# Branch projections of an encoder layer: sums on VectorE, branches joined by an accumulating transfer, weights' parts one product ahead, operands six ahead

## The chip, the cores and the metric

The kernel runs on one core of one Trainium2 chip. The metric is the device time of one execution in microseconds (us); for several executions the median stands. A core has five engines that run side by side, each strictly in its own order: TensorE (PE in the profile) multiplies matrices, VectorE (DVE) and ScalarE (ACT) work element by element, GpSimd (POOL) does so too but can't read the matrix results, and SyncE (SP) issues transfers. Transfers (DMA) can also be issued by ScalarE and GpSimd. Matrix results land in PSUM banks; everything else lies in SBUF tiles of 128 partitions.

## The reference

One encoder layer of width 1024 is applied to two groups (prompt and sample) of 512 tokens each, with the same weights, in float32. After a common input projection there are two branches: a bidirectional mLSTM whose gated output is projected by `w_mo`, and latent attention whose output is projected by `w_ao`. Both are merged by gates and projected once more:

```
y_m = (jax.nn.sigmoid(o) * hm.astype(x.dtype)) @ w_mo
...
y_a = mla_attention(q_nope, q_rope, k_nope, k_rope, va) @ w_ao
...
g_m, g_a = jnp.split(jax.nn.sigmoid(gm), 2, axis=-1)
x = x + (g_m * y_m + g_a * y_a) @ w_out
```

Then follow a normalisation, a SwiGLU feed-forward network (2816 wide) with residual, a gated embedding and a last normalisation.

## The kernel before

Activations lie transposed: one tile holds 128 channels of the 512 tokens of one group, so a group's activation of width 1024 is 8 tiles. Float32 products are made of three matmuls: every operand is split into a high part (a ScalarE cast to fp32r) and a low part (VectorE: the value less its high part, `lo_of`, line 152), and high x high, high x low and low x high are accumulated.

The branch projections, the feed-forward's gate and up projections and its down projection use a scheme of **seven products in place of eight** for a 2 x 2 block product. The four weight blocks are two halves of the contraction by two output tiles; the four operands are two halves of the contraction by the two groups: a and b are the lower half of group 0 and 1, c and d the upper half. The products are called P1, P2, P7, P6, P5, Q4 and P3. Some need sums of operands (`Ops.part`, lines 799 to 819: P7 = b - d, P6 = P7's less a, P5 = a - b, Q4 = P6's plus c, or c - a - d where P6's tile is gone) and sums of weight blocks (`Seven.weights`, lines 861 to 881: P7, P6 and P3, on GpSimd, partly in place). Each product is 12 pairs of weight load and matmul (lines 894 to 896; four tiles of contraction, three matmuls each). `Ops.need` splits the operands of one product; `wsplit` (lines 840 to 845) splits a weight part into one of five buffers, which go round. Results gather in three banks: b1 (P1, P6, P5, P3 one upon the other, copied out by ScalarE between, line 929), b0 (P2) and b2 (P7, Q4). `outputs` (line 923) forms the four result tiles of a quad after P2, P5, Q4 and P3 and hands each to `put`.

`chain` (line 899) writes down the order of products: quad i's P6, P5, Q4, P3 with quad i+1's P1, P2, P7 between them. At each place it asks for operands of this product and the `look` ones after it, makes the quads of this and the next product (which issues their weights' loads from ScalarE, line 855), and emits the product, which first makes its weights' parts. Two chains are run: one of eight quads for the branches (four of `mo` with operands `hops`, then four of `ao` with operands `oops`; line 1018, 862.7 to 1027.8 us of the profile), and one of the feed-forward (`head=True`, from 1154.5 us).

A planner sets each engine's order: it goes over the program with simulated times, and what is emitted earlier has the higher priority among the instructions that are ready. On the chip each engine then keeps that order, whatever the true times are. Where `pinned` is set the order of the text is kept.

For the branches: `put_z` (line 993) multiplies an mLSTM result by its gate and stores it to DRAM (`z1d`); `put_y` (line 1002) loads z back, loads the attention's gate into the tile y, makes y = (y + 1) * t (line 1007) and adds z (line 1008), both on VectorE. Then the sixteen y tiles are halved and split (lines 1026 and 1028), and the output projection (`out_proj`, `proj1`, lines 181 to 183) reads them tile 0 to 7 per group. The operands' sums of `hops` and `oops` run on GpSimd, but for P7's on VectorE. Those of `hops` for P1, P2, P7 and P6 are partly made during the last attention heads (`HOPS`, line 980).

Of the kernel before, what the change touches and what calls it, by code (L numbers as in the profile page):

```python
# [11 lines left out]
ALU = mybir.AluOpType  # L12
# [50 lines left out]
def encoder_kernel(ctx: ExitStack, tc: tile.TileContext, a):  # L63
# [21 lines left out]
    V, S, E, GP = (Engine(e) for e in (nc.vector, nc.scalar, nc.tensor, nc.gpsimd))  # L85
# [277 lines left out]
    for d in range(2):  # L363
        st = R("tr", "mst")
        nc.sync.dma_start(st[:, 0:P], a["mask"][d])
        m = MC.pool.tile([P, P], F32R, name=f"mask{d}")
# [9 lines left out]
    lf, u, z, q = dense("lf"), dense("u"), dense("z"), dense("q")  # L376
# [40 lines left out]
    for i in range(NB):  # L417
        c = slice(i * P, (i + 1) * P)
        V.tensor_tensor_scan(
            out=M[:, c], data0=A[0][:, c], data1=A[0][:, c], initial=mprev[:, i : i + 1], op0=ALU.max, op1=ALU.max  # L420
# [4 lines left out]
    for d in range(1, NB):  # L425
        GP.tensor_copy(out=A[d][:, (NB - d) * P : T], in_=A[0][:, (NB - d) * P : T])
        for j in range(NB - d):
            e = (j + d) * P - 1
            V.tensor_scalar(
                out=A[d][:, j * P : (j + 1) * P],  # L430
                in0=A[d - 1][:, j * P : (j + 1) * P],
# [341 lines left out]
    def load(src, sl=EV, tag="bk", n="ld"):  # L773
        t = sl(tag, n)
        nc.sync.dma_start(t, src)
        return t
# [70 lines left out]
    class Seven:  # L847


        def __init__(self, srcs, kh, ops, out):  # L850
            n = kh * P
            st = []
            for sl, src in zip((WP, WX) if wsn[0] % 4 < 2 else (WX, WP), srcs):
                t = sl("wst", "wst", F32, (P, 1024))
                S.dma_start(t[:, : 2 * n], src)
                st += [t[:, 0:n], t[:, n : 2 * n]]
            wsn[0] += 1
            self.st, self.n, self.kh, self.ops, self.out = st, n, kh, ops, out
            self.bk = {}

        def weights(self, name):
            n, (a11, a12, a21, a22) = self.n, self.st
# [17 lines left out]
                src = a12  # L880
            return wsplit(src)

        def product(self, name):
            whi, wlo = self.weights(name)
            b, first = {"P1": ("b1", 1), "P6": ("b1", 0), "P5": ("b1", 0), "P3": ("b1", 0), "P2": ("b0", 1),
                        "P7": ("b2", 1), "Q4": ("b2", 0)}[name]
            if first:
                self.bk[b] = bank(b)
            bk = self.bk[b]
            sk = dict(skip_group_check=True)  # L890
            for k in range(self.kh):
                c = slice(k * P, (k + 1) * P)
                hi, lo = self.ops.x[name][k]
                E.matmul(bk, whi[:, c], hi, start=bool(first) and k == 0, stop=False, **sk)  # L894
                E.matmul(bk, whi[:, c], lo, start=False, stop=False, **sk)  # L895
                E.matmul(bk, wlo[:, c], hi, start=False, stop=k == self.kh - 1, **sk)  # L896
            self.out(name, self.bk)

    def chain(quads, head=False, look=4):

        order = [(0, n) for n in ("P1", "P2", "P7")]
        if head:
            order = [(0, "P1"), (0, "P2"), (1, "P1"), (1, "P2"), (0, "P7"), (0, "P6"), (0, "P5"), (0, "Q4"), (1, "P7"), (0, "P3")]
        for i in range(1 if head else 0, len(quads)):
            for n in ("P6", "+P1", "P5", "+P2", "Q4", "+P7", "P3"):
                if n[0] != "+":
                    order.append((i, n))
                elif i + 1 < len(quads):
                    order.append((i + 1, n[1:]))
        made = {}  # L910

        def make(i):
            if i not in made:
                made[i] = quads[i][1]()

        for at, (q, n) in enumerate(order):
            for i, m in order[at : at + look + 1]:
                quads[i][0].need(m)
            for i, _ in order[at : at + 2]:
                make(i)  # L920
            made[q].product(n)

    def outputs(put):
# [23 lines left out]
    def load4(src):  # L947
        t = ev4("ld")
        nc.sync.dma_start(t, src)
        return t  # L950
# [6 lines left out]
        raws[0] += 1  # L957
        return load(hzd[g][k], *stage[raws[0] % 4])

    hops = Ops(hraw, None, lambda n: V if n == "P7" else GP)  # L960
    hops.tmp = lambda: None
    units = [(n, [k]) for k in range(4) for n in ("P1", "P2", "P7", "P6")]

# [29 lines left out]
    def put_z(c):  # L993
        def put(at, t):
            cc, g = c + 4 * at[0], at[1]
            m = load4(tmd[g][cc])
            V.scalar_tensor_tensor(out=m, in0=m, scalar=1.0, in1=t, op0=ALU.add, op1=ALU.mult)
            nc.sync.dma_start(z1d[g][cc], m)

        return put  # L1000

    def put_y(c):
        def put(at, t):
            cc, g = c + 4 * at[0], at[1]
            z = load4(z1d[g][cc])
            y = load(tad[g][cc], late["OP"] if c == 0 else X2, "sg" if c == 0 else "x")
            V.scalar_tensor_tensor(out=y, in0=y, scalar=1.0, in1=t, op0=ALU.add, op1=ALU.mult)
            V.tensor_tensor(out=y, in0=y, in1=z, op=ALU.add)
            yr[g][cc] = y

        return put

    oops = Ops(lambda g, k: load(ozd[g][k], X2, "x"), lambda: late["OP"]("ev", "t"), lambda n: V if n == "P7" else GP)

    def pair(kind, c, ops, put):
        return ops, lambda: Seven([a["w8"][W8[f"{kind}{i}"]] for i in (c, c + 4)], 4, ops, outputs(put))

    chain([pair("mo", c, hops, put_z(c)) for c in range(4)] + [pair("ao", c, oops, put_y(c)) for c in range(4)])


    y = [[None] * KD for _ in range(G)]
# [402 lines left out]
```

## Time and profile before

| | us |
|---|---|
| median of 3 runs | 1911.53 (1911.05 to 1914.97) |
| the profiled execution | 1912.25 |
| its span | 1910.5 |
| busy: TensorE / its weight loads | 1845.7 / 1534.8 |
| busy: VectorE, ScalarE, GpSimd | 1240.0, 878.6, 474.4 |

The span runs from the first to the last instruction of the profiled execution. In a row of the timeline stand start, length, engine, line, operation, tiles written and read (out<-in), count, and in brackets how long the engine was idle before and what ended it. In a row of the waits stand who waited for whom, the sum, the number of waits and the longest. In the table by stage, busy time and number of instructions stand for each engine, then the granted clock of TensorE, the share of the DMA engines and their rate. A group's row has its number of instructions, busy time, mean in ns, and the idle time before it by what ended it. Matmuls overlap, so their busy time says less than how far apart they start.

### The profile page before, as it was taken

How to read it: one execution, taken by the hardware profiler on the slowest of the kernel's cores; microseconds unless marked ns; L12 is line 12 of the kernel's file. 1: busy time of each engine (PE TensorE's matmuls, PEld its weight loads, DVE VectorE, ACT ScalarE, POOL GpSimd, SP SyncE). 2: the span in 40 equal slices, each digit the busy share in tenths (PEclk: the TensorE clock that was granted, in tenths of full speed). 3: DMA queues.
4: the chain of work that ended last, by engine and by line, in shares of the span. 5: the costliest groups of instructions: out<-in, count | busy, mean ns of one | idle time of the engine just before them, and what ended most of it. 6: DMA issues, size and time to landing. Idle time of an engine off the chain costs nothing.

```text
span 1910.5 us, 24510 instructions
## 1 busy us (share of the span) xinstructions
PE 1845.7 (97%) x8840; PEld 1534.8 (80%) x8840; DVE 1240.0 (65%) x2134; ACT 878.6 (46%) x1711; POOL 474.4 (25%) x353
## 2 busy tenths in 40 slices
PE   7999999999999999899999988999999999999997
PEld 6898998988888877678777876888888887878886
DVE  7656575836555567976897576444444558778757
ACT  5255555644445566784444345333333344434442
POOL 3000000100000001242540023666565654232100
PEclk9999999999999999999999998999999999999999
DMA  4111101112253123346555331233222336534232
GB/s 163 51 45 34 56 34 56 34 67 72 81 187 121 50 69 122 105 144 215 150 189 179 106 121 64 102 109 112 94 98 93 130 136 222 170 118 143 88 127 88
DMA packets 97881, 207.58 MB, mean 109 GB/s; under 512 B 10656, under 2 KB 21280, under 8 KB 97760
## 3 DMA queue, kind: packets, MB, share of 16 engines
q1 hardware_dynamic: 85664, 163.03, 25.5%
q10 hardware_dynamic: 12096, 43.00, 6.9%
q8 instruction: 69, 1.13, 0.2%
q14 instruction: 52, 0.43, 0.1%
HBM read 151.89 MB, written 54.10 MB: 108 GB/s over the span
## 4 chain that ended last, share of the span: by engine, by line
PE 83%; DVE 9%; issue 3%; ACT 2%; DMA 1%; POOL 1%; SPq 0%; ACTq 0%; DVEq 0%; POOLq 0%
PE b L894 12%; PE b L896 12%; PE b L895 12%; PE mm L181 8%; PE mm L183 8%; PE mm L182 8%; PE nm L580 3%; DVE xl L152 2%; PE mm L79 2%; PE mm L495 2%; PE mm L497 2%; PE mm L496 2%; DVE wp L152 1%; PE pt L759 1%; PE mm L1234 1%
## 5 line engine op out<-in xcount | busy, mean ns | idle before, releaser
L894 PE MATMUL b<-xh,wp 128*128 128x512 f32 x1148 | 444.1, 395 | 19.6 <-ACT em L79 10.2
L895 PE MATMUL b<-xl,wp 128*128 128x512 f32 x1148 | 450.5, 393 | 4.9 <-DVE xl L152 4.9
L896 PE MATMUL b<-xh,wp 128*128 128x512 f32 x1148 | 446.3, 393 | 1.8 <-DVE wp L152 1.6
L843 ACT CAST wp<-wst 128x512 fp32r<-128x512 f32 (+1 forms) x271 | 164.4, 612 | 301.8 <-PE b L896 252.1
L152 DVE TENSOR_TENSOR wp<-wst,wp 128x512 fp32r<-128x512 f32 (+1 forms) x271 | 249.0, 921 | 78.2 <-ACT wp L843 78.0
L894 PEld LDWEIGHTS b<-xh,wp 128*128 128x128 f32 x1148 | 217.0, 189 | 72.6 <-ACT em L79 10.7
L895 PEld LDWEIGHTS b<-xl,wp 128*128 128x128 f32 x1148 | 217.3, 189 | 51.9 <-DVE xl L152 5.3
L896 PEld LDWEIGHTS b<-xh,wp 128*128 128x128 f32 x1148 | 217.3, 189 | 51.3 <-DVE wp L152 3.8
L181 PE MATMUL mm<-hh,whi 128*128 128x512 f32 x592 | 233.4, 395 | 7.3 <-ACT whi L166 7.1
L183 PE MATMUL mm<-hh,wlo 128*128 128x512 f32 x592 | 232.7, 395 | 2.3 <-DVE wlo L152 2.2
L182 PE MATMUL mm<-hl,whi 128*128 128x512 f32 x592 | 233.0, 394 | 0.9 <-DVE hl L277 0.8
L869 POOL TENSOR_TENSOR s<-wst,wst 128x512 f32<-128x512 f32 (+1 forms) x42 | 59.1, 1407 | 416.6 <-DMA wst<-w 282.5
L934 DVE TENSOR_TENSOR u<-b,u 128x512 f32<-128x512 f32 x90 | 61.7, 689 | 139.3 <-PE b L896 85.1
L181 PEld LDWEIGHTS mm<-hh,whi 128*128 128x128 f32 x592 | 112.3, 190 | 31.0 <-ACT whi L166 7.1
L183 PEld LDWEIGHTS mm<-hh,wlo 128*128 128x128 f32 x592 | 112.2, 190 | 26.4 <-DVE wlo L152 3.4
L182 PEld LDWEIGHTS mm<-hl,whi 128*128 128x128 f32 x592 | 112.3, 190 | 25.0 <-DVE hl L277 2.1
L166 ACT CAST whi<-wst 128x1024 fp32r<-128x1024 f32 (+1 forms) x70 | 72.0, 1028 | 102.8 <-PE mm L182 66.7
L152 DVE TENSOR_TENSOR xl<-ld,xh 128x512 fp32r<-128x512 f32 x121 | 97.4, 836 | 10.1 <-ACT xh L827 5.0
L929 ACT COPY u<-b 128x512 f32<-128x512 f32 x90 | 50.9, 588 | 112.3 <-PE b L896 78.8
L152 DVE TENSOR_TENSOR wlo<-wst,whi 128x1024 fp32r<-128x1024 f32 (+1 forms) x70 | 86.4, 1234 | 24.6 <-ACT whi L166 24.4
L152 POOL TENSOR_TENSOR vnl<-avt,vnh 128x512 fp32r<-128x512 f32 x16 | 21.4, 1336 | 283.0 <-ACT vnh L156 260.3
L1176 DVE TENSOR_TENSOR x<-x,b 128x512 f32<-128x512 f32 x84 | 56.6, 681 | 28.5 <-PE b L896 28.1
(332 smaller groups left out, 3590.5 us busy)
## 6 DMA issues: line engine op xcount, KB each, us to landing
wst<-w SPq DMA_DIRECT2D x75, 512.0 KB
wst<-w ACTq DMA_DIRECT2D x60, 512.0 KB
ld<-actd SPq DMA_DIRECT2D x77, 256.0 KB
actd<-t SPq DMA_DIRECT2D x44, 256.0 KB
actd<-sg SPq DMA_DIRECT2D x33, 256.0 KB
x<-x SPq DMA_DIRECT2D x32, 256.0 KB
ld<-hzd SPq DMA_DIRECT2D x32, 256.0 KB
wst<-wd ACTq DMA_DIRECT2D x16, 512.0 KB
```

What stands on the lines that cost most here:

```text
L152: e.tensor_tensor(out=out, in0=src, in1=hi.bitcast(F32), op=ALU.subtract)
L166: S.copy(hi[:, :n], st[:, :n])
L181: E.matmul(bk, whi[:, c], hi, start=k == 0, stop=False)
L182: E.matmul(bk, whi[:, c], lo, start=False, stop=False)
L183: last_mm[0] = E.matmul(bk, wlo[:, c], hi, start=False, stop=k == nk - 1)
L580: E.matmul(bk, l, r, start=n == 0, stop=n == len(terms) - 1)
L843: S.copy(hi, src)
L869: GP.tensor_tensor(out=src, in0=a11, in1=a21, op=ALU.add)
L894: E.matmul(bk, whi[:, c], hi, start=bool(first) and k == 0, stop=False, **sk)
L895: E.matmul(bk, whi[:, c], lo, start=False, stop=False, **sk)
L896: E.matmul(bk, wlo[:, c], hi, start=False, stop=k == self.kh - 1, **sk)
L934: V.tensor_tensor(out=t, in0=b, in1=t, op=ALU.add if name == "P2" else ALU.subtract)
```

## The change

Four edits. `put_y` no longer loads z and adds it on VectorE: GpSimd issues a transfer from `z1d` that adds to the tile y as it lands. The operands' sums of `hops` and `oops` (P6, P5, Q4) move from GpSimd to VectorE. In `chain`, for the branches and the feed-forward alike, quads are made and the weights' parts of this and the next product are prepared (`prep`) ahead of the operands, where before each product made its own parts behind them. The branch chain asks for operands six products ahead, before four.

```diff
-            self.bk = {}
+            self.bk, self.w = {}, {}
...
+        def prep(self, name):
+            if name not in self.w:
+                self.w[name] = self.weights(name)
+            return self.w[name]
+
         def product(self, name):
-            whi, wlo = self.weights(name)
+            whi, wlo = self.prep(name)
...
         for at, (q, n) in enumerate(order):
+            for i, m in order[at : at + 2]:
+                make(i)
+                made[i].prep(m)
             for i, m in order[at : at + look + 1]:
                 quads[i][0].need(m)
-            for i, _ in order[at : at + 2]:
-                make(i)
             made[q].product(n)
...
-    hops = Ops(hraw, None, lambda n: V if n == "P7" else GP)
+    hops = Ops(hraw, None, lambda n: V)
...
             cc, g = c + 4 * at[0], at[1]
-            z = load4(z1d[g][cc])
             y = load(tad[g][cc], late["OP"] if c == 0 else X2, "sg" if c == 0 else "x")
             V.scalar_tensor_tensor(out=y, in0=y, scalar=1.0, in1=t, op0=ALU.add, op1=ALU.mult)
-            V.tensor_tensor(out=y, in0=y, in1=z, op=ALU.add)
+            GP.dma_start(out=y, in_=z1d[g][cc], accum_op=ALU.add)
             yr[g][cc] = y
...
-    oops = Ops(lambda g, k: load(ozd[g][k], X2, "x"), lambda: late["OP"]("ev", "t"), lambda n: V if n == "P7" else GP)
+    oops = Ops(lambda g, k: load(ozd[g][k], X2, "x"), lambda: late["OP"]("ev", "t"), lambda n: V)
...
-    chain([pair("mo", c, hops, put_z(c)) for c in range(4)] + [pair("ao", c, oops, put_y(c)) for c in range(4)])
+    chain([pair("mo", c, hops, put_z(c)) for c in range(4)] + [pair("ao", c, oops, put_y(c)) for c in range(4)], look=6)
```

## The prediction

> **What bounds the kernel now.** First the page, for the engines' shares.
>
> ```profile
> PE 1845.7 (97%) x8840; PEld 1534.8 (80%) x8840; DVE 1240.0 (65%) x2134; ACT 878.6 (46%) x1711; POOL 474.4 (25%) x353
> ```
>
> TensorE bounds nearly all of the run, and the change takes no matmul away. It can win only time in which TensorE waits, or runs slowly after a wait. So next the waits of TensorE.
>
> ```profile
> PE b L894 <- ACT em L79: 10.2, 1, 10.2
> PE mm L181 <- ACT whi L166: 7.1, 1, 7.1
> PE b L895 <- DVE xl L152: 4.9, 1, 4.9
> PE b L894 <- ACT u L929: 4.6, 9, 1.7
> ```
>
> The first lies at the entry of the feed-forward network (1154.5 us), the second ahead of everything that changes. The third lies in the branch projections. Third, a table by stage: attention's end, projections (two stretches), the feed-forward's steady part, its passage to the down projection.
>
> ```profile
> core 0: us, PE busy (x) PEld busy (x) DVE busy (x) ACT busy (x) POOL busy (x), PEclk, DMA share, GB/s
> 745.00:863.00 118.00, 106.64 (x515) 84.17 (x514) 97.37 (x203) 90.06 (x184) 39.20 (x30) 1.00 0.41 133
> 863.00:925.00 62.00, 62.00 (x273) 50.93 (x272) 45.82 (x60) 29.03 (x53) 16.39 (x11) 1.00 0.61 208
> 925.00:970.00 45.00, 38.41 (x159) 30.89 (x158) 42.01 (x48) 19.68 (x36) 31.55 (x18) 0.92 0.60 185
> 1175.00:1555.00 380.00, 378.39 (x1650) 308.95 (x1649) 175.03 (x205) 135.69 (x236) 216.52 (x145) 1.00 0.29 99
> 1555.00:1615.00 60.00, 56.82 (x235) 45.35 (x234) 48.62 (x58) 31.39 (x57) 35.44 (x23) 0.95 0.70 237
> ```
>
> Matmuls per us tell more than busy shares: 273 in 62 us are 4.40 per us unhindered. At that rate the 159 of 925 to 970 need 36.1 us, so **8.9 us are lost** there, with VectorE busy 42.0 of 45 and POOL 31.6. In the feed-forward 1650 in 380 us are 4.34 per us; the 235 of 1555 to 1615 need 54.1 us, so **5.9 us are lost** there. These two stretches are what the change can reach. The timeline shows the first one:
>
> ```profile
> 950.22 0.40 PE L895 MATMUL b<-xl,wp 128*128 128x512 f32 x1
> 955.52 0.80 PE L895 MATMUL b<-xl,wp 128*128 128x512 f32 x1 [4.90 <-DVE xl L152]
> 956.11 1.06 PE L896 MATMUL b<-xh,wp 128*128 128x512 f32 x2
> 956.97 0.63 PE L894 MATMUL b<-xh,wp 128*128 128x512 f32 x1
> ```
>
> After the wait two matmuls take 0.86 us (956.11 to 956.97), 0.43 each, against 62/273 = 0.227: idleness has slowed the clock too. The awaited operand stands on VectorE at 953.72:
>
> ```profile
> 931.07 2.49 DVE L805 TENSOR_TENSOR t<-ld,ld 128x512 f32<-128x512 f32 x4
> ...
> 953.72 1.75 DVE L152 TENSOR_TENSOR xl<-t,xh 128x512 fp32r<-128x512 f32 x1
> ```
>
> Four such operations in a row take 2.49 us (0.62 each) while POOL is idle; beside POOL one takes 1.75. At 0.62 the 48 operations of this stretch need 29.9 us, not 42.0: about 12 us are waiting for POOL. The Trainium skill ("SBUF — State Buffer", section "SBUF: two separate sides") calls the pair of ports that VectorE and GpSimd share an exclusive lock, held for a whole instruction, for an operation with two SBUF inputs beside a GpSimd one that reads SBUF. The trace agrees: 1.75 against 0.62.
>
> **The change part by part.**
>
> *Sums from POOL to VectorE.* These groups of POOL (745 to 1030 us) go, all but the weights' sums, which are other lines:
>
> ```profile
> L811 POOL TENSOR_TENSOR ld<-ld,ld 128x512 f32<-128x512 f32 x8 | 12.3, 1538 | 7.6 <-DMA ld<-hzd 7.6
> ...
> L808 POOL TENSOR_TENSOR t<-t,ld 128x512 f32<-128x512 f32 x4 | 8.2, 2072 | 5.6 <-DVE xl L152 5.6
> L814 POOL TENSOR_TENSOR t<-t,ld 128x512 f32<-128x512 f32 x4 | 6.9, 1725 | 0.0
> L818 POOL TENSOR_TENSOR ld<-ld,ld 128x512 f32<-128x512 f32 x4 | 5.2, 1324 | 0.0
> L808 POOL TENSOR_TENSOR ld<-ld,ld 128x512 f32<-128x512 f32 x4 | 5.1, 1286 | 35.0 <-PE pt L759 19.9 <-issue 6.6 <-DVE mx L749 6.0
> L817 POOL TENSOR_TENSOR ld<-ld,ld 128x512 f32<-128x512 f32 x4 | 5.0, 1278 | 0.0
> ```
>
> They are 28 sums; at 0.62 they are 17.4 us more for VectorE. Twelve (L808 on t, half of L811, L814) lie in 925 to 970: 8.2 + 6.15 + 6.9 = 21.2 of POOL's 31.55 us. So two thirds of the 12 us of waiting go (8 us), and 12 x 0.62 = 7.4 us come. In itself this is a draw in VectorE's load. What it mends is latency: an operand no longer goes to POOL at 1.7 us and back, and the late ones need not queue behind stretched ones.
>
> *Branches added by the transfer.* Sixteen additions leave VectorE:
>
> ```profile
> L1008 DVE TENSOR_TENSOR ld<-ld,ld x16: 678/685/1746, 952.0 to 1030.4; 128x512 f32<-128x512 f32 x16
> ```
>
> At 0.62 that is 9.9 us over the chain's end, little of it before 970. Also 16 plain loads of z and their tiles go; 16 transfers issued by POOL take their place, each waiting for the product in line 1007. Behind it POOL has only the weights' sums; before, such a sum ran at 988.77 and its cast at 1001.36:
>
> ```profile
> 988.77 1.28 POOL L869 TENSOR_TENSOR s<-wst,wst 128x512 f32<-128x512 f32 x1 [8.27 <-DMA wst<-w]
> ```
> ```profile
> 1001.36 0.62 ACT L843 CAST wp<-s 128x512 fp32r<-128x512 f32 x1
> ```
>
> Those 12.6 us less its 1.28 are the cover for a held POOL queue; I cost it at nothing. The last transfer has no cover. The chain's end now:
>
> ```profile
> 1027.56 0.39 PE L896 MATMUL b<-xh,wp 128*128 128x512 f32 x1
> ```
> ```profile
> 1027.98 0.69 DVE L934 TENSOR_TENSOR u<-b,u 128x512 f32<-128x512 f32 x1 [1.30 <-PE b L896]
> ...
> 1030.44 0.69 DVE L1008 TENSOR_TENSOR ld<-ld,ld 128x512 f32<-128x512 f32 x1
> ```
> ```profile
> 1031.17 4.80 ACT L1026 ACTIVATE yh<-ld 128x512 fp32r<-128x512 f32 x9 [4.81 <-DVE ld L1008]
> ```
> ```profile
> 1032.55 0.39 PE L181 MATMUL mm<-yh,whi 128*128 128x512 f32 x1
> ```
>
> That last matmul is the output projection's 22nd (the first follows at 1027.56 + 0.227, 21 more steps make 1032.55), the first that reads the last branch tile. The tile is cast from 1031.17 and split: ready about 1032.5, with no slack. An accumulating transfer isn't in this trace. Its nearest rows are plain transfers, a quiet and a crowded one:
>
> ```profile
> 750.78 2.78 DMA ld<-hzd
> ```
> ```profile
> 1603.70 5.16 DMA ld<-actd
> ```
>
> With POOL's part between nothing and one of its sums (1.28), the tile comes 2.78 - 0.69 = 2.1 to 5.16 + 1.28 - 0.69 = 5.8 us later. The lower end is nearer (DMA queues are thin by then); I take 3. The planner can put the other group's first matmuls (21 x 0.227 = 4.8 us, which need no late tile) ahead, so the cost on TensorE is between 0 and 5.8; I take 2. The Trainium skill ("DMA: Bandwidth & Descriptors", "Anatomy of one DMA — SWDGE (gpsimd) path") has 2.0 us + bytes/436e3 for a transfer issued by GpSimd. For 256 KB that would be 2.6 us, by which the tile would be 1.9 us late and not 3; no run here shows it.
>
> *Weights' parts one product ahead.* Weights of product n+1 now stand ahead of the operands of n+4 (n+6 in the branches) in the planner's order, in both chains. In the steady feed-forward nothing changes, since a cast waits for its buffer and not for its turn:
>
> ```profile
> L843 ACT CAST wp<-wst 128x512 fp32r<-128x512 f32 (+1 forms) x271 | 164.4, 612 | 301.8 <-PE b L896 252.1
> ```
>
> Most of ScalarE's idleness ahead of it (252.1 of 301.8 us) ends when TensorE gives one of the five buffers back. In the passage the order matters:
>
> ```profile
> 1606.65 0.62 ACT L1169 CAST xh<-ld 128x512 fp32r<-128x512 f32 x1 [6.37 <-DMA ld<-actd]
> 1607.17 1.14 ACT L843 CAST wp<-wst 128x512 fp32r<-128x512 f32 x2
> ```
> ```profile
> 1607.84 0.50 PE L894 MATMUL b<-xh,wp 128*128 128x512 f32 x1 [2.48 <-ACT wp L843]
> ```
>
> ScalarE held two weights' casts behind an operand that was still in a transfer and is needed only products later. With weights first, up to the whole 5.9 us goes; but the planner counts with its own transfer times, so the order may stay: 0 to 5.9, I take 3. The 10.2 us at 1154.5 wait for a copy of the embedding's stage, whose order is pinned: nothing.
>
> *Operands six ahead.* Two products (24 x 0.227 = 5.4 us) more in which VectorE can do the 28 splits and 16 sums of the second branch. With the sums it takes most of the 8.9 us; I take 7 of it, since VectorE stays near nine tenths busy (42.0 - 8 + 7.4 = 41.4 of 45, now spread over 50.4: 0.82).
>
> *Attention's end.* 16 of the 28 sums (9.9 us) join VectorE in 745 to 863, where it is busy 97.4 of 118. POOL's contention goes in part. Between 1 us won and 2 lost; I take 0.5 lost.
>
> **Sum.** -7 - 3 + 2 + 0.5 = **-7.5 us**. The profiled execution took 1912.25 us (span 1910.5), 0.7 over the runs' median of 1911.53; its waits are taken to stand in all runs. So 1911.53 - 7.5 = 1904.0.
>
> **Rivals.**
> 1. *Both stalls go whole and the tail is filled*: -8.9 - 5.9 + 0.5 = -14.3, 1897.2. For it: each has one visible cause that the change removes. Against: both stretches are crowded, and a late operand tends to be followed by the next.
> 2. *The stall moves*: VectorE stays the bound in 925 to 970, since its load is a draw. Then 3 of 8.9 us are won, nothing in the passage, the tail takes 2 and attention 0.5: -0.5, 1911.0, no change. For it: 41.4 us of load in 45. Against: the two products more.
> 3. *POOL's queue blocks, slower*: each of the 16 transfers waits on POOL for its product and holds the weights' sums of the next products. With 10 us won in the two stretches and 0.5 lost in attention, slower by over 0.2% (3.8 us) needs 13.3 us, 0.83 us per transfer; at 1 us each, tail among them, the sum is +6.5, 1918.0. For it: POOL runs strictly in order, and P7, P6 and P3 all need it. Against: the 12.6 us of cover above.
> 4. *Half clock at the tail*: if the tile is 5.8 us late and nothing fills in, the idleness also slows about ten matmuls by 0.2 us each, as after 955.52: +7.8 in place of +2, in all -1.7, 1909.8, no change. The Trainium skill ("TensorE: Matmul & The Clock Gate", Part 1) halves the clock after an idle window of about 3.4 us; 4.90 us here agrees.
>
> **Chances.** Forecast 0.47; rival 1 0.15; rival 2 0.18; rival 4 0.07; rival 3 0.13. A measurement of this kernel can tell about 0.2%, 3.8 us. Faster by more than that is forecast and rival 1: 0.62; within it rivals 2 and 4: 0.25; slower: 0.13. The range reaches from a little over rival 1 (1896.5, attention 0.7 better) to the forecast without the passage's 3, with 3 of 7 in the projections and the tail's 5.8: 1911.5 - 3 + 5.8 + 0.5 = 1914.8, taken to 1914.
>
> **What would show it.** Right: in the projections' crowded stretch no wait of TensorE over 2 us on xl; VectorE's mean there under 0.75 us; POOL without L808, L811, L814; the wait on the weights' cast in the passage gone. At the output projection's start a wait on yh or the line-1007 tile of some 2 us shows the tail. The forecast is wrong if waits on VectorE in the projections still sum to 5 us, if TensorE waits for weights whose sum POOL held back, or if the feed-forward's entry moves by more than 3 us.

## The result and the profile after

The changed kernel takes 1924.93 us (median of 4 runs, 1921.33 to 1925.85); the kernel before took 1911.29 us beside it (4 runs, 1911.04 to 1914.97). The ratio is 1.0055, with a 95% interval of 1.0041 to 1.0068: slower by half a per cent, where 1904.0 us and faster was forecast. The profiled execution took 1925.45 us with a span of 1923.6. In the changed kernel the three matmuls of a product stand in lines 899 to 901 (before 894 to 896), the bank copies u in 935 and 940, `put_y`'s product in 1012, the accumulating transfer in 1013, the halving casts yh and yl in 1031 and 1033.

The engines' line of the page, then the five largest waits of TensorE:

```profile
PE 1854.3 (96%) x8840; PEld 1539.4 (80%) x8840; DVE 1235.6 (64%) x2146; ACT 878.3 (46%) x1711; POOL 454.2 (24%) x341
```
```profile
PE mm L181 <- ACT whi L166: 10.1, 3, 7.4
PE b L899 <- ACT em L79: 9.8, 1, 9.8
PE b L899 <- ACT u L935: 5.1, 9, 2.2
PE b L899 <- ACT wp L843: 4.5, 3, 2.5
PE pj L181 <- DVE mx L749: 4.3, 1, 4.3
```

The wait on xl (4.9 us) is gone, as forecast. In its place stand two more waits on the weights' cast whi (together 2.7 us, both in the output projection; the 7.4 us lie at the start of the run, as the 7.1 before), a longer wait on the softmax column mx (4.3 against 2.9) and more on the weights' parts wp. TensorE is busy 8.6 us longer for the same 8840 matmuls: part of them ran at a slower clock, half of the full one by the spacing shown below. The table by stage, each stretch moved along with its work:

```profile
core 0: us, PE busy (x) PEld busy (x) DVE busy (x) ACT busy (x) POOL busy (x), PEclk, DMA share, GB/s
745.00:871.00 126.00, 111.70 (x510) 87.72 (x509) 105.23 (x219) 89.00 (x182) 18.77 (x14) 0.95 0.39 125
871.00:933.00 62.00, 62.00 (x272) 50.91 (x272) 46.76 (x64) 30.88 (x57) 17.28 (x11) 1.00 0.60 208
933.00:978.00 45.00, 41.10 (x177) 32.74 (x177) 42.98 (x62) 20.48 (x37) 18.50 (x9) 1.00 0.63 204
1188.00:1568.00 380.00, 378.39 (x1650) 308.88 (x1649) 169.97 (x206) 135.74 (x236) 217.55 (x145) 1.00 0.29 99
1568.00:1628.00 60.00, 56.95 (x242) 45.55 (x241) 47.88 (x58) 31.34 (x57) 35.84 (x23) 0.97 0.68 236
```

The crowded stretch of the projections does 177 matmuls in 45 us, before 159. VectorE does 62 operations there in 42.98 us, 0.69 each, before 48 in 42.01 (0.88): POOL holds it up far less, as forecast. Five of them still take 1.77 to 1.79 us beside POOL's sums of weights. Attention's end takes 8 us more for the same work, at a mean clock of 0.95 instead of 1.00.

Where the first matmul of each stage starts by the timeline, and how long the stages are (the output projection from its first matmul to the start of its last):

| us | before | after | difference |
|---|---|---|---|
| start to the first branch product | 862.7 | 871.1 | +8.4 |
| branch projections | 165.1 | 163.5 | -1.6 |
| output projection | 92.4 | 99.5 | +7.1 |
| to the feed-forward's first product | 34.4 | 34.0 | -0.4 |
| feed-forward | 649.8 | 648.6 | -1.2 |
| rest of the span | 106.2 | 107.0 | +0.8 |

The sum is +13.1 us, the difference of the two spans. So two places lose 15.5 us, and the branch projections, which were to win 7, win 1.6. Each column is one execution.

**Attention's end.** TensorE's last waits there, and the first branch product, before:

```profile
857.28 0.66 PE L759 MATMUL pt<-ident,p 128*128 128x128 f32 x4 [0.86 <-DVE apl L152]
858.25 0.66 PE L759 MATMUL pt<-ident,p 128*128 128x128 f32 x4 [0.32 <-DVE apl L152]
859.59 0.50 PE L766 MATMUL av<-aph,vnh 128*128 128x512 f32 x1 [0.68 <-ACT aph L761]
...
862.73 0.39 PE L894 MATMUL b<-xh,wp 128*128 128x512 f32 x1
```

and after:

```profile
862.58 0.66 PE L759 MATMUL pt<-ident,p 128*128 128x128 f32 x4 [1.20 <-DVE apl L152]
864.16 1.12 PE L759 MATMUL pt<-ident,p 128*128 128x128 f32 x4 [0.93 <-DVE apl L152]
865.95 0.79 PE L766 MATMUL av<-aph,vnh 128*128 128x512 f32 x1 [0.67 <-ACT aph L761]
866.54 0.63 PE L767 MATMUL av<-aph,vnl 128*128 128x512 f32 x1
866.97 0.63 PE L768 MATMUL av<-apl,vnh 128*128 128x512 f32 x1
...
871.07 0.39 PE L899 MATMUL b<-xh,wp 128*128 128x512 f32 x1
```

From the last block of 12 value products to the first branch product 3.1 us passed before (859.59 to 862.73), now 5.1 (865.95 to 871.07): the matmuls follow each other at 0.43 us, half the clock. The same spacing stands at two earlier places of attention in the changed kernel, 765.1 to 768.5 and 799.2 to 802.6 us, and nowhere in attention before: some 23 steps, so by an estimate 4.5 us (23 x 0.2) of the whole 8.4. VectorE shows why the last blocks come late:

```profile
848.06 0.67 DVE L811 TENSOR_TENSOR ld<-ld,ld 128x512 f32<-128x512 f32 x1
848.66 0.68 DVE L748 TENSOR_REDUCE mx<-sc 128x1 f32<-128x512 f32 x1
849.26 0.14 DVE L749 TENSOR_SCALAR mx<-mx 128x1 f32<-128x1 f32 x1
849.32 0.67 DVE L811 TENSOR_TENSOR ld<-ld,ld 128x512 f32<-128x512 f32 x1
849.92 0.68 DVE L817 TENSOR_TENSOR ld<-ld,ld 128x512 f32<-128x512 f32 x1
```

The moved sums (L811, L817, L818) stand between the steps of the softmax (mx, apl), which TensorE waits for. They are needed only products later, but VectorE takes them where the planner put them.

**The output projection.** The last branch tile, from VectorE to the transfer and to ScalarE:

```profile
1036.47 0.68 DVE L1012 SCALAR_TENSOR_TENSOR ld<-ld,u 128x512 f32<-128x512 f32 x1
```
```profile
1037.56 0.87 POOL L1013 DMA_DIRECT2D ld<-z1d  x1 [3.62 <-DVE ld L1012]
```
```profile
1042.26 4.28 ACT L1031 ACTIVATE yh<-ld 128x512 fp32r<-128x512 f32 x8 [9.22 <-DMA ld<-z1d]
1046.45 1.03 ACT L166 CAST whi<-wst 128x1024 fp32r<-128x1024 f32 x1
1047.38 0.63 ACT L1031 ACTIVATE yh<-ld 128x512 fp32r<-128x512 f32 x1
1047.91 1.03 ACT L166 CAST whi<-wst 128x1024 fp32r<-128x1024 f32 x1
```
```profile
1047.53 0.50 PE L181 MATMUL mm<-yh,whi 128*128 128x512 f32 x1 [1.96 <-ACT whi L166]
...
1049.00 0.79 PE L181 MATMUL mm<-yh,whi 128*128 128x512 f32 x1 [0.74 <-ACT whi L166]
```

ScalarE sits idle for 9.22 us until one tile lands at 1042.26. Behind that cast stand seven others, none of which waits any more, and then the casts of the weights of the projection's third and fourth columns. TensorE doesn't wait for the tile: it had two columns of other work. It waits for the weights (2.7 us in two), and then runs at half clock to 1055. The same happens some 15 us earlier:

```profile
1025.68 1.15 ACT L1031 ACTIVATE yh<-ld 128x512 fp32r<-128x512 f32 x2 [3.12 <-DMA ld<-z1d]
1026.73 0.56 ACT L935 COPY u<-b 128x512 f32<-128x512 f32 x1
```
```profile
1027.35 0.50 PE L899 MATMUL b<-xh,wp 128*128 128x512 f32 x1 [2.24 <-ACT u L935]
```

Here a bank copy u stands behind a cast that waits for a landing, and the bank isn't free for the next product. Behind this wait too the matmuls are 0.43 us apart, until 1031.

**The projections' crowded stretch.** Three short waits took the place of the long one:

```profile
965.11 0.50 PE L899 MATMUL b<-xh,wp 128*128 128x512 f32 x1 [0.57 <-ACT u L935]
969.78 0.47 PE L899 MATMUL b<-xh,wp 128*128 128x512 f32 x1 [1.66 <-DVE u L940]
977.69 0.50 PE L899 MATMUL b<-xh,wp 128*128 128x512 f32 x1 [1.67 <-ACT wp L843]
```
```profile
977.02 1.66 ACT L843 CAST wp<-wst 128x512 fp32r<-128x512 f32 x3 [7.67 <-DMA wst<-w]
```

The last of them waits for a load of weights that was issued at 970.87 and landed at 977.00.

**The passage to the down projection** keeps its wait:

```profile
1621.55 0.61 PE L899 MATMUL b<-xh,wp 128*128 128x512 f32 x1 [2.52 <-ACT wp L843]
```

### The profile page after: what moved, and what is told of

Read it like the earlier page. It is cut to its first block, busy times and chain, and to the rows that moved or that the text cites. A ratio compares the mean times of both kernels' runs of the same rounds, so it can differ in the third digit from the quotient of the medians.

```text
span 1923.6 us, 24521 instructions
## 1 busy us (share of the span) xinstructions
PE 1854.3 (96%) x8840; PEld 1539.4 (80%) x8840; DVE 1235.6 (64%) x2146; ACT 878.3 (46%) x1711; POOL 454.2 (24%) x341
## 4 chain that ended last, share of the span: by engine, by line
PE 78%; DVE 10%; issue 4%; DMA 3%; ACT 3%; POOL 1%; SPq 0%; ACTq 0%; DVEq 0%; POOLq 0%
PE b L899 11%; PE b L901 10%; PE b L900 10%; PE mm L181 8%; PE mm L183 8%; PE mm L182 8%; PE nm L580 3%; DVE xl L152 2%; PE mm L79 2%; PE mm L495 2%; PE mm L497 2%; PE mm L496 2%; DVE wp L152 1%; PE pt L759 1%; PE mm L1239 1%
## 5 line engine op out<-in xcount | busy, mean ns | idle before, releaser
L152 DVE TENSOR_TENSOR wp<-wst,wp 128x512 fp32r<-128x512 f32 (+1 forms) x271 | 243.7, 901 | 82.5 <-ACT wp L843 81.9
L166 ACT CAST whi<-wst 128x1024 fp32r<-128x1024 f32 (+1 forms) x70 | 71.9, 1027 | 106.7 <-PE mm L182 69.5
```

Of the source, the lines that this page charges most:

```text
L152: e.tensor_tensor(out=out, in0=src, in1=hi.bitcast(F32), op=ALU.subtract)
L166: S.copy(hi[:, :n], st[:, :n])
```

## The experiments

One theory and its rivals. *Order*: the change puts work that isn't urgent, or that waits for a landing, ahead of urgent work on an engine that keeps its order, the sums on VectorE at attention's end and the casts on ScalarE at the output projection; what it wins in the projections is lost again, and more. Its rivals: the transfers cost by their issue and traffic; the landing is simply too late for TensorE; the weights' parts one ahead or the operands six ahead crowd the engines. Each ratio is against runs of the kernel before on the same chip (its medians there were 1913.36, 1913.04, 1914.6 and 1914.37 us). "First product" is the start of the first branch product; stage lengths are read as in the table above. They come from one profiled execution of each kernel; the median and the ratio come from all its runs.

**Four times, one edit undone in the changed kernel.** Without the accumulating transfer:

```diff
+            z = load4(z1d[g][cc])
             y = load(tad[g][cc], ...)
...
-            GP.dma_start(out=y, in_=z1d[g][cc], accum_op=ALU.add)
+            V.tensor_tensor(out=y, in0=y, in1=z, op=ALU.add)
```

> All of the change, but z is loaded and added on VectorE as before. Theory (the sum of the loss is attention's end plus the accumulating transfer): the transfer's 4.7 us of landing stands at the head of ScalarE's order, with the copy of a bank and two weights' casts behind it. Without it the output projection's matmuls take 92 to 93 us again (after: 99.5), the wait of 2.6 us ahead of the branches' last products shrinks to about 1.1, and the time falls by 8 to 11 us to 1914 to 1917. Rival (weights one ahead and operands six ahead have spoilt the planner's order at the output projection): it still takes over 97 us and the time stays above 1921.

Measured: 1914.79 us, ratio 1.0008 (0.9998 to 1.0018). Branches 159.0 us (from 163.5), output projection 93.5 (from 99.5): 10.5 us come back, in the two stages where ScalarE waited for landings. First product unmoved at 872.3.

The first branch's sums back on GpSimd:

```diff
-    hops = Ops(hraw, None, lambda n: V)
+    hops = Ops(hraw, None, lambda n: V if n == "P7" else GP)
```

> All of the change, but the first branch's operand sums (16) are on GpSimd again. Theory: these sums stand between the softmax's steps in VectorE's order at the end of attention; without them the first branch product starts at 862 to 864 us (after: 871.1), and the time falls by 7 to 9 us to 1916 to 1918. Rival (weights' parts or operands asked for earlier push the attention aside): the first branch product still starts after 868, and the time stays above 1922.

Measured: 1919.79 us, ratio 1.0030 (1.0014 to 1.0045). First product at 865.5 us (from 871.1): 5.6 us of the 8.4 come back. What is left is half clock (matmuls 0.43 us apart at 798 to 803 and 861 to 864 us): TensorE's waits from 740 to 875 us sum to 10.6 us, against 14.0 in the change and 11.2 before. The branches take 165.7 us here (from 163.5), with a wait of 2.5 us on a weights' part, the output projection 98.5.

The weights' parts behind the operands again:

```diff
-            for i, m in order[at : at + 2]:
-                make(i)
-                made[i].prep(m)
             for i, m in order[at : at + look + 1]:
                 quads[i][0].need(m)
+            for i, _ in order[at : at + 2]:
+                make(i)
```

> All of the change, but the weights' parts and the quads are made behind the operands again. Theory: it does next to nothing, since a weight part waits for its buffer: 1922 to 1927, the feed-forward's matmuls within 1 us of after. Rival (it hurts the branches, by casts ahead of copies, or makes the late load of weights at 977 us): 3 us or more faster. Forecast's old reason (it helps): 3 us or more slower.

Measured: 1924.58 us, ratio 1.0047 (1.0031 to 1.0063). Feed-forward 649.8 us (from 648.6), output projection 99.8: nothing that can be told from the change.

The operands four ahead again (`look=6` left out):

> All of the change, but the branches ask for operands four products ahead. Theory: the sums for Q4 of the first quad are asked for two products later and leave attention's end in part, which wins 2 to 4 us there; in the second branch's operands waits on VectorE come back by 1 to 3 us: 1921 to 1926. Rival (six ahead is the cause of attention's loss): the first branch product starts before 865 and the time is below 1918.

Measured: 1922.08 us, ratio 1.0043 (1.0028 to 1.0058). Branches 160.0 (from 163.5), first product 872.5, output projection 99.5. The wait on the weights' part at 977.69 isn't there in this execution. Six ahead wins nothing here; the interval overlaps that of the change.

**Four times, one edit alone in the kernel before**: the accumulating transfer, the first branch's sums on VectorE, the second branch's sums on VectorE, and the weights one ahead (the lines of the change's diff, one at a time).

> The kernel before with the accumulating transfer alone. Theory (the transfer costs by itself: landing at the head of ScalarE's and VectorE's orders): output projection 98 to 100 us, the last products 1 to 3 us late, 7 to 11 us slower than before. Rival (it costs only with the planner's order of the whole change): output projection under 95 us, under 3 us slower.

Measured: 1924.66 us, ratio 1.0051 (1.0034 to 1.0068): branches 169.0 (from 165.1), output projection 99.5 (from 92.4). Alone it costs what it costs in company.

> The kernel before with the first branch's operand sums on VectorE alone. Theory: attention's end is 6 us longer (first branch product 868 to 870 us), 4 to 7 us slower. Rival (they hurt only beside weights one ahead and operands six ahead): first branch product before 865, within 2 us of before.

Measured: 1921.92 us, ratio 1.0039 (1.0026 to 1.0052): first product at 871.3, branches 165.0, output projection 93.9 (before 92.4).

> The kernel before with the second branch's operand sums on VectorE alone. Theory: this is the part that pays: attention as before, the branches' products 5 to 7 us shorter (before 165.1 from the first product to the output projection), waits on xl gone at 955: 4 to 7 us faster. Rival (the gain came from six ahead or from weights one ahead): branches within 2 us of before.

Measured: 1908.63 us, ratio 0.9972 (0.9960 to 0.9984): branches 159.4 (from 165.1). First product at 865.1: 2.3 us later than before, though attention was to stay as it was; matmuls 0.43 us apart stand at 861 to 864. This one line is the part of the change that pays.

> The kernel before with weights' parts one product ahead alone. Theory: casts of weights enter attention's end, which costs 2 to 3 us there, and the feed-forward stays as it is (649 to 650 us, the wait for the weights' cast near 1607 us still there): 0 to 3 us slower. Rival (the forecast's): the wait at 1607 goes and the feed-forward is 3 us or more shorter.

Measured: 1913.56 us, ratio 1.0005 (0.9992 to 1.0017): feed-forward 649.4 (from 649.8), first product 862.5. The forecast's 3 us in the passage aren't there. The output projection takes 94.7 us (from 92.4) with nothing changed in it, 2.0 of it half clock by the spacing: so much one execution can differ from another.

**The late tile's cast behind the others.** The change, with the halving casts written in another order; TensorE's own order stays.

```diff
-    for g in range(G):
-        for k in (0, 4, 1, 5, 2, 6, 3, 7):
+    for g, ks in ((0, (0, 4, 1, 5, 2, 6, 3)), (1, (0, 4, 1, 5, 2, 6, 7, 3)), (0, (7,))):
+        for k in ks:
```

> The whole change, but ScalarE's cast of the branch tile that lands last (group 0, row 7) is written behind the other group's eight casts instead of ahead of them. TensorE's order stays: it does 42 matmuls of two columns (9.5 us) before it needs that tile. Theory S (ScalarE's order): in the changed kernel the landing at 1042.26 us is in itself early enough; what costs is that seven ready casts and the casts of the third and fourth column's weights stand behind it. Then the output projection goes from 99.5 us to 92 to 95, the wait of TensorE on the weights' cast whi (10.1 us in three) goes below 6, and the time falls by 4 to 7 us to a ratio of 1.002 to 1.0035 against the kernel before. Rival L (the landing itself): the tile is late for TensorE; then the output projection stays at 98 to 100 us, the waits become waits on yh or yl of that tile, and the ratio stays at 1.005 to 1.006.

Measured: 1920.66 us, ratio 1.0033 (1.0021 to 1.0045). The output projection takes 95.8 us, a little over the expected 92 to 95; the branches take 166.2 (from 163.5). The waits of TensorE from 1015 to 1130 us:

```profile
PE b L899 <- ACT u L935: 4.7, 2, 4.0
...
PE mm L181 <- ACT whi L166: 0.7, 2, 0.5
```

In the changed kernel the waits on whi from 1034 us on were:

```profile
PE mm L181 <- ACT whi L166: 2.7, 2, 2.0
```

Of these 2.7 us 0.7 are left, with all sixteen transfers kept and their tile as late as ever. The expected sum of below 6 over the whole run wasn't reached (7.8): 7.1 of it stand at the start of the run, where nothing changes, and should not have been counted. So the landing wasn't too late for TensorE; the cast that waits for it stood too early in ScalarE's line. The wait on the bank copy u (4.0 us) is still there, and longer than in the change (2.2).

**Only the last four tiles added as before.**

```diff
+            z = load4(z1d[g][cc]) if c == 3 else None
...
-            GP.dma_start(out=y, in_=z1d[g][cc], accum_op=ALU.add)
+            if c == 3:
+                V.tensor_tensor(out=y, in0=y, in1=z, op=ALU.add)
+            else:
+                GP.dma_start(out=y, in_=z1d[g][cc], accum_op=ALU.add)
```

> The whole change, but the last four of the sixteen branch tiles are added by a load and a VectorE addition as before; the first twelve keep the accumulating transfer. Taking all sixteen away won 10 us (output projection 93.5, branches 159.0 us). Theory S: only the tiles at the end cost, since only there do ScalarE's casts stand in line behind a landing; then the output projection falls to 92 to 95 us, the branches to 159 to 161, and the ratio comes to 1.000 to 1.002. Rival T (each transfer costs, by its issue on POOL or its traffic): twelve of sixteen stay, so only a quarter to a half of the 10 us goes, 2.5 to 5 us, and the ratio stays at 1.003 to 1.0045.

Measured: 1916.39 us, ratio 1.0012 (1.0002 to 1.0023). The output projection is whole again (92.8 us). The branches are not: 162.7, against 159 to 161 expected; TensorE still waits 3.4 us near 1027 for a bank copy that stands behind the casts of the third quad's tiles. So it isn't only the last four tiles that cost; the casts of the quad before them do too, where a bank copy stands behind them.

**The casts behind the last bank copy.** All sixteen transfers are kept. The scale of four late casts is read from a column that is made from the last copy u, so that they can't stand ahead of it; group 0's last tile comes behind the other group's, as above.

```diff
+    V.tensor_scalar(out=half[:, 0:1], in0=ulast[0][:, 0:1], scalar1=0.0, scalar2=0.5, op0=ALU.mult, op1=ALU.add)
...
-            S.activation(out=hi, in_=t, func=AF.Copy, scale=0.5)
+            S.activation(out=hi, in_=t, func=AF.Copy, scale=half[:, 0:1] if g == 0 and k % 4 >= 2 else 0.5)
```

> The whole change with all sixteen accumulating transfers, but ScalarE's casts of group 0's last branch tiles stand behind the last bank copy u (their scale is read from a column that is made from that copy), and the cast of the tile that lands last stands behind the other group's. Theory S (all that the transfers cost is ScalarE's order: bank copies and weights' casts in line behind casts that wait for a landing): the wait of TensorE on u of 3.6 to 4.4 us near 1027 goes as well, branches 159 to 161 us (from 163.5), output projection 92 to 96 us (from 99.5), ratio 1.000 to 1.002, like the change without the transfers (1.0008). Rival T (part of it is the transfers' issue and traffic): branches stay at 162 to 164, ratio 1.0025 to 1.004.

Measured: 1919.39 us (1913.69 to 1920.13), ratio 1.0022 (1.0012 to 1.0031), between the two theories. In the profile (an execution of 1914.76 us) the branches take 158.7 us and the wait on u is down to 0.7. ScalarE, then TensorE:

```profile
1026.29 3.74 ACT L1036 ACTIVATE yh<-ld 128x512 fp32r<-128x512 f32 x7
...
1036.83 0.72 ACT L1036 ACTIVATE yh<-ld,mx 128x512 fp32r<-128x512 f32 x1 [4.30 <-DMA ld<-z1d]
```
```profile
1037.61 0.73 PE L181 MATMUL mm<-yh,whi 128*128 128x512 f32 x2 [0.73 <-ACT yh L1036]
```

ScalarE still waits for the landing, but with nothing urgent behind it. TensorE now waits for the tile itself, 0.73 us. The output projection takes 96.0 us, against 93.5 without any transfer. By the stages that is 8.3 of the transfers' 10.5 us; but this execution is 4.6 us below its median, and one part of its gain isn't the edit's: the load of weights that TensorE waited for at 977 in the change lands in 4.6 us here (968.28 to 972.88) instead of 6.1, and the wait of 1.67 us is not there. By the ratios (1.0055, 1.0022, and 1.0008 without transfers) some 6 of 9 us were ScalarE's order. The 2 to 3 us that stay with the transfers are not settled: the last two intervals overlap.

**The same, with the first branch's sums on GpSimd**, which leaves of the two costs only that rest.

> The kernel of the run before, with the first branch's sums back on GpSimd as well: the change with its two costs mended and nothing else undone. If the two costs are all that made the change slower, it does what the change without them does: 1906 to 1911 us, ratio 0.996 to 0.9985, first branch product at 865 to 866.5 us, branches 159 to 161. Rival: a third cost is left (the waits of TensorE on u and on wp in the projections, which the whole change has and the kernel before has not), then branches 162 to 165 and ratio 0.999 to 1.001.

Measured: 1911.18 us, ratio 0.9984 (0.9973 to 0.9995), faster than the kernel before and at the slow end of what was expected. Beside the run above, taken on the same chip and different in these sums alone, it is 8.2 us faster (1919.39 to 1911.18): that is the price of the first branch's sums on VectorE by the medians. First product 866.0, branches 158.3, output projection 96.9. No third cost in the branches; what keeps it behind the versions without transfers (below) is mostly the output projection.

**Attention's end in two halves**, in the kernel before: first only the four P6 sums on VectorE, then only the twelve of P5 and Q4.

```diff
-    hops = Ops(hraw, None, lambda n: V if n == "P7" else GP)
+    hops = Ops(hraw, None, lambda n: V if n in ("P7", "P6") else GP)
```

> The kernel before with only the four P6 sums of the first branch (745 to 800 us) on VectorE; its twelve others (843 to 858 us) stay on POOL. All sixteen cost 8.5 us at the first branch product. Theory E (the end): the cost comes from the twelve that stand among the last softmax steps; then the four cost 0 to 1.5 us, first branch product at 862.5 to 864.5, ratio 0.999 to 1.001. Rival W (VectorE's load): the cost goes with the number of sums, so a quarter or more, 2 to 4 us, first product at 865 to 867, ratio 1.001 to 1.002.

Measured: 1915.16 us, ratio 1.0009 (1.0000 to 1.0019). First product at 866.8; attention as a whole began 1.7 us later in this execution (first value product at 622.1, before 620.4), so 2.4 us are left. The wait on mx is longer (4.3 us, before 2.9), but TensorE's waits from 740 to 875 us sum to no more than before (10.8 against 11.2). What is new is half clock at 767 to 770 and 801 to 804 us. Runs with the four on POOL show half clock in attention too, so the 2.4 us can't all be put down to the edit; by the median and the ratio the four cost nothing to 3.6 us. Both theories stay possible.

```diff
+    hops = Ops(hraw, None, lambda n: GP if n == "P6" else V)
```

> The kernel before with the twelve first-branch sums of 843 to 858 us on VectorE, and the four P6 sums (745 to 800 us) on POOL. The four alone cost 2.4 us at the first branch product. If the two places simply add, the twelve cost 5 to 7 us: first product at 867.5 to 870, ratio 1.0015 to 1.003. Rival: the slow clock behind the run of short waits comes only when both are there; then the twelve cost 2 to 4 us and no matmuls at 0.43 us stand at 866 to 871.

Measured: 1919.2 us, ratio 1.0027 (1.0016 to 1.0038). First product at 870.2, and the same last waits as in the change (1.19, 0.93 and 0.68 us). Two stretches tell the parts of attention's end apart; each row is one execution, with the three times in brackets:

| us | from the third last block of 12 value products to the last | from there to the first branch product |
|---|---|---|
| before (843.09, 859.59, 862.73) | 16.5 | 3.1 |
| four on VectorE (847.18, 863.67, 866.82) | 16.5 | 3.1 |
| change, all sixteen back on POOL (844.63, 861.11, 865.49) | 16.5 | 4.4 |
| twelve on VectorE (844.11, 865.08, 870.23) | 21.0 | 5.2 |
| change (844.96, 865.95, 871.07) | 21.0 | 5.1 |

Over all the profiles the first length is 16.5 to 16.7 us in the nine kernels with the twelve sums on POOL, and 20.5 to 21.0 in the nine with them on VectorE. So the twelve cost 4.0 to 4.5 us there, whatever else is changed. The second length is 3.1 to 3.2 at full clock and 4.2 to 5.2 at half; half clock stands there in eight of the nine kernels with the twelve on VectorE and in three of the nine without. So the twelve alone bring the late end, and the slow clock more often; the rival that needs both halves falls. By the ratios the halves nearly add up (0.0009 and 0.0027, both together 0.0039).

**What is left when both costs are left out**: the kernel before with the second branch's sums on VectorE and the operands six ahead, with and without the weights one ahead.

> The kernel before with the second branch's sums on VectorE, the weights one product ahead and the operands six ahead; the branches are added by load and VectorE, and the first branch's sums stay on POOL. Theory: the second branch's sums are what pays (4.4 us alone), the one-ahead weights are worth 0, and six ahead at most 2: 1906 to 1910 us, ratio 0.9965 to 0.9985. Rival: the three need each other, as the forecast had it (10 us won in the two stretches): 1900 to 1904 us, ratio 0.993 to 0.995. Other rival: one-ahead and six-ahead load VectorE and ScalarE at the wrong place, and the gain is gone: ratio 0.999 to 1.001.

Measured: 1906.47 us, ratio 0.9961 (0.9948 to 0.9974); branches 158.9.

> The kernel before with the second branch's sums on VectorE and its operands six ahead, without the weights one product ahead. With all three it took a ratio of 0.9961, with the sums alone 0.9972. Theory that one-ahead is worth nothing anywhere: 0.995 to 0.998, with branches 158 to 160 us, as with it. Rival (one-ahead is worth 2 us beside six-ahead): 0.997 to 0.999 and branches 160.5 to 162.

Measured: 1908.23 us, ratio 0.9966 (0.9954 to 0.9977); branches 160.5. Both are 0.3 to 0.4% faster than the kernel before, with intervals clear of 1; neither differs from the sums alone (0.9972) by more than the intervals. That the three need each other isn't borne out (1900 to 1904 us were expected for it).

## Why the prediction was wrong

**Attention's end is the first step that failed**: "Between 1 us won and 2 lost; I take 0.5 lost." It was 8.4 lost in the profile, 8.5 with this edit alone, and 8.2 by the medians of the two runs that differ in it only. The step compared VectorE's load with its capacity (97.4 us busy of 118) and found room. But VectorE had no room where the sums went: the planner put twelve of them into the last 15 us, between softmax steps that follow each other without slack. A free share over 118 us says little about a chain in which each step waits for the one before. The runs put 4.0 to 4.5 us on the twelve as TensorE's late blocks; most of the rest is half clock (an estimate of 4.5 us in the changed kernel's profile, at three places). That part is not a fixed price: it comes with longer waits more often, and without the edit at times. What the four near 764 us cost stays open.

**The tail is the second**: "the cost on TensorE is between 0 and 5.8; I take 2", and a held POOL queue "at nothing"; for ScalarE the sum has no term. The last tile was late by about what was thought: product done at 1037.15, landed at 1042.26, 5.1 us, where the addition took 0.69; 4.4 us late lies within the forecast's 2.1 to 5.8. TensorE had as much other work as the forecast's better case gave it, 42 matmuls. What failed is that the forecast asked who is queued behind the waiting instruction on POOL, and not on ScalarE, which casts the tile. There the seven other casts, the weights of two columns and, earlier, a bank copy stood behind it: 7.1 us in the output projection and, with 163.5 against 158.7 us, 4.8 in the branches. Of the 4.8 the late load of weights is 1.7, so some 3 are ScalarE's line (1.5 more wait on u and the half clock behind it). That is close to rival 4's place and sign (a late tile and half clock) but not its mechanism, since TensorE didn't wait for the tile. Rival 3's, POOL's queue, cost TensorE nothing that its waits show. Of the two sums of weights for P7 that POOL makes beside the transfers (963 to 1040 us), the first waited 12.51 us for its load; the second did stand behind a transfer's issue, for whose product POOL sat idle 5.48 us, but from 978 us to the output projection TensorE waits for no weights' part:

```profile
977.14 1.27 POOL L869 TENSOR_TENSOR s<-wst,wst 128x512 f32<-128x512 f32 x1 [12.51 <-DMA wst<-w]
...
993.24 0.86 POOL L1013 DMA_DIRECT2D ld<-z1d  x1 [5.48 <-DVE ld L1012]
993.80 1.63 POOL L869 TENSOR_TENSOR s<-wst,wst 128x512 f32<-128x512 f32 x1
```

**The projections' 7 us were right in size, and in cause but for one part**, and hidden by the above: with ScalarE's order mended the branches take 158.7 us, 6.4 less than before, and without transfers 159.0. The second branch's sums do nearly all of it alone (159.4), not the operands six ahead, which the step gave a share.

**The passage's 3 us failed.** The wait (2.52 us) stands as it did (2.48). The forecast itself said that the planner's order might stay; with the weights one ahead alone nothing moved (649.4 against 649.8 us). Why the planner keeps the operand's cast ahead there wasn't tried.

With the measured terms the sum is +8.4 (attention) - 6.4 (projections) + 4.8 + 7.1 (ScalarE's line, the transfers and the late load) - 0.8 (the rest) = +13.1 us. It closes because each term is a difference between stages of the same profiles; half clock, which varies from one execution to the next, is in several of them. Of the signs that the forecast named, three came (no long wait on xl, VectorE's mean under 0.75, the three lines gone from POOL). The passage's didn't, and the tail's came in another place: ScalarE waited for the tile (9.22 us), TensorE did not. "The feed-forward's entry moves by more than 3 us", which was to make the forecast wrong, came true, by 13.5.

## What to carry to other kernels

Before moving work to an engine with idle time, look at what stands ahead of and behind it in that engine's own order at that place, above all where short steps of several engines hand on to each other; the idle share of the stage is no measure of room there. Where an operation is replaced by a longer wait, ask who first touches its result and what that engine has queued behind: the price is paid by that queue, even if the final consumer has time. And test the parts of a change one by one: here one line was worth 5 us (0.28%), hidden under the 7 to 9 us each (0.39 and 0.47%) of two others.

## What the runs showed of the hardware

**An accumulating transfer.** The sixteen issues of 256 KB each, from the view of the tile's name:

```profile
L1013 POOL DMA_DIRECT2D ld<-z1d x16: 860/876/1542, 963.6 to 1037.6; - x16
```
```profile
DMA to landing us min/median/max: 3.9/4.7/7.3
```

An issue holds POOL for 0.88 us (the median), and the addition stands in SBUF 4.7 us after it (3.9 to 7.3). The Trainium skill ("DMA: Bandwidth & Descriptors", "Anatomy of one DMA — SWDGE (gpsimd) path") has a formula for a transfer issued by GpSimd, which makes an estimate of 2.6 us for 256 KB; the accumulating one took nearly twice that, and the measured figure stands.

**The clock after short waits.** The wait on mx near 764 us was 2.9 us before and left the clock alone. In the changed kernel it is longer:

```profile
764.27 0.50 PE L181 MATMUL pj<-cqh,whi 128*128 128x512 f32 x1 [4.34 <-DVE mx L749]
...
765.09 0.63 PE L181 MATMUL pj<-cqh,whi 128*128 128x512 f32 x1
765.52 0.63 PE L182 MATMUL pj<-cql,whi 128*128 128x512 f32 x1
```

The matmuls behind it are 0.43 us apart. That is as the Trainium skill has it ("TensorE: Matmul & The Clock Gate", Part 1: half clock after an idle window of about 3.4 us). Over the profiles, half clock follows this wait in all nine kernels where it is 3.7 to 4.4 us (the four sums on VectorE), and in three of the nine where it is 2.9 to 3.4 us; 3.18 us brought it once, and 3.42 left it out once. But at 865.95 no wait was over 1.20 us; three of them (1.20, 0.93, 0.67) with a few small transposes between stood ahead of half clock. In the run with the casts behind the last bank copy the same three waits (1.20, 0.93, 0.68) left it at full clock. And in the change with the first branch's sums back on GpSimd, the waits are those of the kernel before (0.84, 0.32, 0.68 against 0.86, 0.32, 0.68), and half clock came all the same:

```profile
861.11 0.79 PE L766 MATMUL av<-aph,vnh 128*128 128x512 f32 x1 [0.68 <-ACT aph L761]
861.71 0.63 PE L767 MATMUL av<-aph,vnl 128*128 128x512 f32 x1
862.13 0.63 PE L768 MATMUL av<-apl,vnh 128*128 128x512 f32 x1
```

Here the measured rows decide over the page's window: behind short waits half clock comes in some executions and not in others, and 1 to 2 us of difference between two executions can be this alone.
